# Layer 0's MLP with row weights split one pair ahead and TensorE's order written for all eight first pairs; VectorE's order written at the end of the attention output projection

## The chip, the cores and the metric

The kernel runs on one core of one Trainium2 chip. A core has five engines that work in parallel, each on its own list of instructions in order, and wait for each other by semaphores: TensorE (PE in the profile; its weight loads are PEld), VectorE (DVE), ScalarE (ACT), GpSimd (POOL) and SyncE (SP, which here only issues DMAs). The metric is device time in microseconds (us). Before the change it is 1701.62 us, the median of three runs (1700.1 to 1701.74).

## The reference, cut to what matters

Two sequences of 512 tokens and width 1024 go through the same two layers. Layer 0 mixes tokens by a Fourier transform, layer 1 by attention; each layer ends with a squared-ReLU MLP of width 4096.

```python
def sq_relu_mlp(h, w_up, w_down):
    a = jnp.maximum(h @ w_up, 0)
    return (a * a) @ w_down

def trunk(x, ...):
    for i in range(DEPTH):
        if i % N_MIXERS == 0:
            x = x + fourier_mix(rms_norm(x, fourier_norm[j]), fourier_w_out[j])
        else:
            x = x + gqa_attention(rms_norm(x, attn_norm[j]), ...)
        x = x + sq_relu_mlp(rms_norm(x, mlp_norm[i]), mlp_w_up[i], mlp_w_down[i])
    return rms_norm(x, final_norm)
```

The change touches how the first MLP starts, and how the second MLP's input is prepared at the end of attention's output projection (`o @ w_o`, added to `x`).

## The kernel before, in words

**Matmuls in three parts.** Every float32 operand is split into a high and a low half of type float32r: ScalarE casts the high half (L82), VectorE subtracts it from the original to get the low half (L83). A product of two operands is then three matmuls: high by high, high by low, low by high (L869 in `product`). The first two of the three need only the weight's high half, the third needs its low half. One `product` runs over four 128-blocks, so it is 12 matmuls.

**The MLP's up-projection by pairs.** `first_product(l, blocks, rows, ahead)` takes the 32 blocks of 128 hidden units two at a time, as a *pair*, and uses a seven-product scheme on 2 by 2 blocks (sequences by halves of the width). The activations stand in `blocks.b` under seven names: `b11` and `b21` (sequence 0), `b22`, and the sums `t1` to `t4`. The first two products of a pair, `first()` with `b11` and `second()` with `b21`, need only sequence 0 and the pair's row weights (`row`, loaded by `load`, split by `split_row`). `second()` accumulates into the same PSUM tile as `first()`, after ScalarE has copied `first()`'s result out (L903). The other five are in `rest()`: `t2`, `t3`, `t1`, then `t4` accumulated on the PSUM tile of `t3`, then `b22` accumulated on that of `t1`. VectorE reads each of these tiles before the next product goes on top of it: L947 after `t2`, L951 after `t3`, L960 after `t1`, L969, L978.

Because `b12`, `b22` and the sums come later (they need sequence 1), the kernel runs the first two products of `AHEADS[l]` pairs ahead: eight pairs in layer 0 (p = 0 to 7), six in layer 1. The first four pairs of layer 0 come with their weights already split (`rows`). For pairs 4 to 7 the loop at L1017 loads and splits, runs `first()`, then `second()` of the pair before. Between them, `todo` (a generator, `Blocks.second_sums`) prepares the sums of the activations: normalization (L208), subtractions (L266, L267, L271, L278) and splits (L82, L83). At p = 5 and 6 the loop also prepares pair 0's weight sums (L918, L919, L922, later L930).

**Buffers.** Loaded weights go to tiles `raw` (5 buffers), split weights to `w` (4 buffers), activations to `u` (38), temporaries to `t` (8), results to `ps` (8 PSUM banks). A load can be issued only when a `raw` buffer has been given back by the split that read it.

**What sets the order.** A scheduler places the instructions of each engine, by its own estimate of when operands are there, and the order on each engine is fixed when the program is built. `tc.manual_schedule(engines={...})` keeps the instructions of the named engines within its block in the order in which the code writes them; instructions of other blocks may still come between. In layer 0's loop TensorE's order is written for p = 0 to 4 and left to the scheduler for p = 5 to 7.

**The end of the output projection.** For the second half of the heads (kh = 1), the loop at L1639 computes, for each sequence q and each of eight row blocks fo, 12 matmuls (L77 to L79, `mm3`) and adds them to `x` (VectorE L852, reading PSUM). Then `square` (ScalarE L154, GpSimd adds it to a running sum, L156), `blocks.gain` (ScalarE L196), and every second fo a store (`put_away`). While sequence 1 is at fo = 4 to 7, the four chunks c0 to c3 of sequence 0 are made ready for layer 1's MLP: `blocks.first(c)` normalizes (VectorE L208) and casts the high half (ScalarE L219); `blocks.first_lo(c)` makes the low half (VectorE L224). c0 and c1 are `b11`, c2 and c3 are `b21`. The MLP's first matmuls follow right behind the last project.

Of the kernel before, what the change touches and what calls it, by code (L numbers as in the profile page):

```python
# [40 lines left out]
def trunk_kernel(ctx, tc, x_in, xt_in, y_out, dcos, dsin, feat, rope, gfour, gcol, grow, gfin,  # L41
# [22 lines left out]
    def tm(shape=(P, 512), dt=F32):  # L64
        return tmp.tile(list(shape), dt, tag="t2", name=nm("t"))
# [4 lines left out]
    def ps():  # L70
        return psp.tile([P, 512], F32, tag="ps", name=nm("ps"))
# [4 lines left out]
    def mm3(out, lh, ll, rh, rl, first, last):  # L76
        nc.tensor.matmul(out, lh, rh, start=first, stop=False)  # L77
        nc.tensor.matmul(out, lh, rl, start=False, stop=False)  # L78
        nc.tensor.matmul(out, ll, rh, start=False, stop=last)  # L79
# [30 lines left out]
    def load_w(src, eng=nc.vector, parts=1, home=own):  # L110
        raw = load_raw(src)
        w = home()
        for i in range(parts):
            sl = slice(i * 1024 // parts, (i + 1) * 1024 // parts)
            split(w[0][:, sl], w[1][:, sl], raw[:, sl], eng)
        return w
# [24 lines left out]
    def load_xs(q, src):  # L141
        for i in range(4):
            xs[q, i] = slot([P, 2, 512], F32)
            nc.sync.dma_start(xs[q, i], src[i])

    def xt(q, fo):
        return xs[q, fo // 2][:, fo % 2]

    def square(q, fo, n=512):

        if fo == 0:
            acc[q] = tm()
        s = tm() if fo else acc[q]
        nc.scalar.activation(s[:, :n], xt(q, fo)[:, :n], AF.Square)  # L154
        if fo:
            nc.gpsimd.tensor_add(acc[q][:, :n], acc[q][:, :n], s[:, :n])  # L156
# [25 lines left out]
    def put_away(q, i):  # L182
        nc.sync.dma_start(park[q, i], xs[q, i])
# [482 lines left out]
    ET = mybir.EngineType  # L666
    with tc.manual_schedule(engines={ET.PE, ET.Activation, ET.DVE, ET.Pool, ET.SP}):
# [127 lines left out]
        blocks = Blocks(0)  # L795
# [26 lines left out]
        rows = []  # L822
# [49 lines left out]
    def first_product(l, blocks, rows, ahead):  # L872
# [8 lines left out]
        np_, ah = NPS[l], AHEADS[l]  # L881
# [133 lines left out]
        pairs = [Pair(p) for p in range(np_)]  # L1015
        whole = 2 * np_ == NF
        for p in range(ah):  # L1017
            pair = pairs[p]
            with tc.manual_schedule(engines={ET.PE}) if whole and p < 5 else nullcontext():
                if p < len(rows):  # L1020
                    pair.row = rows[p]
                else:
                    pair.load()
                    pair.split_row()
                pair.first()
                if whole:
                    if p == 3:
                        blocks.root(1)
                        pairs[0].second()
                        pairs[1].second()  # L1030
                        blocks.spread(1)
                        pairs[2].second()
                    elif p > 3:
                        pairs[p - 1].second()
                else:
                    if p > 0:
                        pair.second()
                    if p == 1:
                        pairs[0].second()
                    if p == 2:  # L1040
                        blocks.root(1)
                    if p == 3:
                        blocks.spread(1)
            if p > 3 - whole:
                for _ in range(3 - 2 * l):
                    next(todo, None)
            if whole and p == ah - 1:
                pair.second()
            if 2 * np_ == NF and p == 5:
                pairs[0].load_sums()  # L1050
                pairs[0].sums_23()
            if 2 * np_ == NF and p == 6:
                pairs[0].split_23()
# [62 lines left out]
    def second_product(l, blocks, rows, late=lambda: None, ready=lambda m: None):  # L1116
# [179 lines left out]
        def finish(m):  # L1296
            left[m] -= 1
            if left[m] == 0:
                nc.vector.tensor_add(xs[0, m][:, 1], xs[0, m][:, 1], e[m])
                nc.vector.tensor_add(xs[1, m], xs[1, m], e[m].unsqueeze(1).broadcast_to([P, 2, 512]))  # L1300
                ready(m)

        first_product(l, blocks, rows, ahead)
        e += [tm() for _ in range(4)]
        items, waiting = [], []
# [181 lines left out]
    vt, kr, kT, qr, oT = {}, {}, {}, {}, {}  # L1487
# [70 lines left out]
    for cg in (2, 0, 1):  # L1558
        ws = wkv if cg == 2 else [load_w(w_qkv[cg, u], home=own if u < 2 else lent) for u in range(4)]
# [71 lines left out]
    blocks = Blocks(2 * KC)  # L1631
    nc.scalar.activation(one[:, :1], last[:, :1], AF.Sqrt)
    for kh in range(2):
        ahead += [load_w(w_o[k], home=lent) for k in range(len(ahead), 4 * kh + 4)]
        ws = ahead[4 * kh :]
        for q in range(NSEQ):
            if kh == 0:
                load_xs(q, park[q])
            for fo in range(KC):  # L1639
                project(q, fo, ws, [(oT[q, 4 * kh + k][:, 0], oT[q, 4 * kh + k][:, 1]) for k in range(4)])  # L1640
                if kh == 0:
                    continue
                square(q, fo)
                blocks.gain(q, fo)
                if fo % 2:
                    put_away(q, fo // 2)
                if (q, fo) == (1, 1):
                    blocks.root(0)
                if (q, fo) == (1, 3):
                    blocks.spread(0)  # L1650
                if (q, fo) > (1, 3):
                    blocks.first(fo - 4)
                if (q, fo) > (1, 4):
                    blocks.first_lo(fo - 5)
    blocks.first_lo(3)
    second_product(1, blocks, ())
    ats = []
# [5 lines left out]
    ws = [load_w(w_down[f]) for f in range(NF - 2 * NPS[1])]  # L1663
# [266 lines left out]
```

## Time and profile before

| what | value |
|---|---|
| three runs | 1701.62, 1701.74, 1700.1 us |
| profiled execution's own time | 1699.59 us |
| its span, first to last instruction | 1697.8 us |
| TensorE's granted clock, mean | 0.999 |
| VectorE busy | 1234.2 us (73%) |
| ScalarE busy | 854.9 us (50%) |
| GpSimd busy | 333.4 us (20%) |
| mean DMA traffic | 157 GB/s |
| layer 0's MLP, first matmul | 96.25 us |
| layer 1's MLP, first matmul | 1060.83 us |

All stretches of time below are in microseconds from the start of the span. In a timeline each row has: start, duration, engine, line of the kernel, operation, output and inputs, shape, and a count where rows were merged; in brackets the idle time of the engine just before, and what ended it.

### The profile page before, as it was taken

How to read it: one execution, taken by the hardware profiler on the slowest of the kernel's cores; microseconds unless marked ns; L12 is line 12 of the kernel's file. 1: busy time of each engine (PE TensorE's matmuls, PEld its weight loads, DVE VectorE, ACT ScalarE, POOL GpSimd, SP SyncE). 2: the span in 40 equal slices, each digit the busy share in tenths (PEclk: the TensorE clock that was granted, in tenths of full speed). 3: DMA queues.
4: the chain of work that ended last, by engine and by line, in shares of the span. 5: the costliest groups of instructions: out<-in, count | busy, mean ns of one | idle time of the engine just before them, and what ended most of it. 6: DMA issues, size and time to landing. Idle time of an engine off the chain costs nothing. (4 is left out here: it accounts for less than half of the span.)

```text
span 1697.8 us, 21868 instructions
## 1 busy us (share of the span) xinstructions
PE 1681.2 (99%) x7845; PEld 1395.0 (82%) x7845; DVE 1234.2 (73%) x1809; ACT 854.9 (50%) x1487; POOL 333.4 (20%) x304
## 2 busy tenths in 40 slices
PE   9999999999999999999999999999999999999998
PEld 7987888888788888788888888788888888888887
DVE  8788776557887879876588744687755479787864
ACT  7566444456242424457787714654444544344234
POOL 1321443221000000232344303014422200000002
PEclk9999999999999999999999999999999999999999
DMA  9643555449454644611000213335544686555322
GB/s 337 169 149 113 197 189 182 151 169 390 173 201 146 216 143 175 227 53 34 18 25 1 100 60 127 104 120 195 183 143 154 224 310 229 164 207 189 124 75 100
DMA packets 103679, 265.81 MB, mean 157 GB/s; under 512 B 10177, under 2 KB 10177, under 8 KB 103570
## 3 DMA queue, kind: packets, MB, share of 16 engines
q1 hardware_dynamic: 87410, 232.69, 39.4%
q10 hardware_dynamic: 14256, 25.96, 4.0%
q0 software_dynamic: 1904, 5.77, 1.7%
q8 instruction: 61, 1.00, 0.2%
q14 instruction: 48, 0.39, 0.1%
HBM read 189.40 MB, written 73.92 MB: 155 GB/s over the span
## 5 line engine op out<-in xcount | busy, mean ns | idle before, releaser
L869 PE MATMUL ps<-u,w 128*128 128x512 f32 x4656 | 1065.8, 389 | 4.9 <-DVE w L83 2.5
L869 PEld LDWEIGHTS ps<-u,w 128*128 128x128 f32 x4656 | 872.4, 188 | 189.7 <-DVE w L83 4.1
L82 ACT CAST w<-raw 128x1024 fp32r<-128x1024 f32 (+1 forms) x224 | 217.4, 981 | 444.1 <-PE ps L869 261.4
L83 DVE TENSOR_TENSOR w<-raw,w 128x1024 fp32r<-128x1024 f32 (+1 forms) x224 | 255.1, 1142 | 59.5 <-ACT w L82 59.0
L156 POOL TENSOR_TENSOR t<-t,t 128x512 f32<-128x512 f32 (+1 forms) x56 | 77.6, 1385 | 737.2 <-ACT t L154 681.3
L83 DVE TENSOR_TENSOR u<-u,u 128x1024 fp32r<-128x1024 f32 (+1 forms) x131 | 156.2, 1219 | 21.3 <-ACT u L82 20.6
L82 ACT CAST u<-u 128x1024 fp32r<-128x1024 f32 (+1 forms) x131 | 131.5, 1044 | 72.4 <-PE ps L869 48.8
L77 PE MATMUL ps<-u,u 128*128 128x512 f32 (+2 forms) x388 | 150.2, 387 | 0.4 <-DVE u L83 0.4
L1135 DVE TENSOR_TENSOR u<-ps,u 128x512 f32<-128x512 f32 x160 | 109.5, 686 | 54.0 <-PE ps L869 53.2
L79 PE MATMUL ps<-u,u 128*128 128x512 f32 (+2 forms) x388 | 144.4, 372 | 0.0
L78 PE MATMUL ps<-u,u 128*128 128x512 f32 (+2 forms) x388 | 144.2, 372 | 0.0
L869 PE MATMUL ps<-u,u 128*128 128x512 f32 x576 | 137.6, 390 | 0.6 <-DVE t L960 0.5
L869 PEld LDWEIGHTS ps<-u,u 128*128 128x128 f32 x576 | 107.9, 188 | 24.1 <-issue 0.9
L986 POOL TENSOR_TENSOR u<-u 128x512 f32<-128x512 f32 x28 | 36.6, 1309 | 401.4 <-ACT u L885 401.4
L83 DVE TENSOR_TENSOR u<-ps,u 128x512 fp32r<-128x512 f32 (+4 forms) x118 | 74.7, 649 | 19.6 <-ACT u L82 18.5
L79 PEld LDWEIGHTS ps<-u,u 128*128 128x128 f32 x388 | 73.1, 188 | 13.0
L77 PEld LDWEIGHTS ps<-u,u 128*128 128x128 f32 x388 | 73.3, 189 | 10.7 <-DVE u L83 0.6
L78 PEld LDWEIGHTS ps<-u,u 128*128 128x128 f32 x388 | 73.4, 189 | 10.5
L82 ACT CAST u<-ps 128x512 fp32r<-128x512 f32 (+4 forms) x118 | 65.6, 561 | 27.1 <-PE ps L79 11.6
L947 DVE TENSOR_TENSOR t<-ps,u 128x512 f32<-128x512 f32 x30 | 20.7, 690 | 79.8 <-PE ps L869 58.0
L852 DVE TENSOR_TENSOR u<-ps,u 128x512 f32<-128x512 f32 (+1 forms) x48 | 30.9, 645 | 64.4 <-PE ps L79 64.4
L77 PE MATMUL ps<-u,w 128*128 128x512 f32 (+2 forms) x192 | 65.1, 339 | 0.0
(244 smaller groups left out, 1987.0 us busy)
## 6 DMA issues: line engine op xcount, KB each, us to landing
raw<-w_up SPq DMA_DIRECT2D x82, 512.0 KB, 4.5
u<-spill_t SPq DMA_DIRECT2D x60, 512.0 KB, 5.9
raw<-w_sum SPq DMA_DIRECT2D x56, 512.0 KB, 4.3
u<-spill_b SPq DMA_DIRECT2D x45, 512.0 KB, 5.2
spill_t<-u SPq DMA_DIRECT2D x87, 256.0 KB, 2.0
spill_b<-t ACTq DMA_DIRECT2D x60, 256.0 KB, 3.0
raw<-w_row SPq DMA_DIRECT2D x28, 512.0 KB, 4.1
park<-u SPq DMA_DIRECT2D x24, 512.0 KB, 3.2
```

The source lines that it names most:

```text
L77: nc.tensor.matmul(out, lh, rh, start=first, stop=False)
L78: nc.tensor.matmul(out, lh, rl, start=False, stop=False)
L79: nc.tensor.matmul(out, ll, rh, start=False, stop=last)
L82: nc.scalar.copy(dst_hi, src)
L83: eng.tensor_sub(dst_lo, src, f32(dst_hi))
L156: nc.gpsimd.tensor_add(acc[q][:, :n], acc[q][:, :n], s[:, :n])
L852: nc.vector.tensor_add(x[:, :n], o[:, :n], x[:, :n])
L869: nc.tensor.matmul(o, w[x][:, sl], h[k][y], start=first and k + i == 0, stop=k == n - 1 and i == 2, skip_group_check=not first)
L947: nc.vector.tensor_add(u2, ob, t[:, 0])
L986: eng.tensor_sub(t[:, 0], b12, b11)
L1135: nc.vector.tensor_add(x, o, x)
```

## The change

Two edits. In `first_product`, for layer 0: the block in which TensorE's order is written now covers all eight pairs (p = 0 to 7); pair 4 is loaded and split at its own turn, and pairs 5, 6 and 7 one turn earlier, at the end of the turn of the pair before; and `second()` of the last pair moves from behind the block (and behind a step of `todo`) into it. At the end of the output projection: for sequence 1 and fo = 4 to 7, VectorE's order is the written one, and `first_lo` of the chunk before is written ahead of `first` of the next chunk.

```diff
         for p in range(ah):
             pair = pairs[p]
-            with tc.manual_schedule(engines={ET.PE}) if whole and p < 5 else nullcontext():
+            with tc.manual_schedule(engines={ET.PE}) if whole else nullcontext():
                 if p < len(rows):
                     pair.row = rows[p]
-                else:
+                elif not whole or p == len(rows):
                     pair.load()
                     pair.split_row()
                 pair.first()
...
                     elif p > 3:
                         pairs[p - 1].second()
+                    if len(rows) <= p < ah - 1:
+                        pairs[p + 1].load()
+                        pairs[p + 1].split_row()
+                    if p == ah - 1:
+                        pair.second()
...
-            if whole and p == ah - 1:
-                pair.second()
...
             for fo in range(KC):
-                project(q, fo, ws, [(oT[q, 4 * kh + k][:, 0], oT[q, 4 * kh + k][:, 1]) for k in range(4)])
-                if kh == 0:
-                    continue
-                square(q, fo)
-                blocks.gain(q, fo)
...
-                if (q, fo) > (1, 3):
-                    blocks.first(fo - 4)
-                if (q, fo) > (1, 4):
-                    blocks.first_lo(fo - 5)
+                with tc.manual_schedule(engines={ET.DVE}) if (kh, q) == (1, 1) and fo > 3 else nullcontext():
+                    project(q, fo, ws, [(oT[q, 4 * kh + k][:, 0], oT[q, 4 * kh + k][:, 1]) for k in range(4)])
+                    if kh == 0:
+                        continue
+                    square(q, fo)
+                    blocks.gain(q, fo)
...
+                    if (q, fo) > (1, 4):
+                        blocks.first_lo(fo - 5)
+                    if (q, fo) > (1, 3):
+                        blocks.first(fo - 4)
```

How many instructions each engine has does not change. Their order changes in two stretches only, on each engine; GpSimd's order does not change at all. On SyncE the load of pair 6's row weights now stands ahead of the two loads for pair 0's weight sums, where it stood behind them; the second of these two and a store change places; pair 7's load stays behind them.

**VectorE in layer 0's MLP.** In the kernel before, VectorE has these rows from pair 5's weights (`w_1462`) to pair 6's (`w_1518`); ahead of them, between the split of `w_1417` (pair 4) and here, stand L930 and six rows on activations.

```order
L83 TENSOR_TENSOR w_1462<-raw_1460,w_1462 128x1024
L83 TENSOR_TENSOR u_1410<-u_1406,u_1409 128x1024
L266 TENSOR_TENSOR u_1452<-u_1131,u_885 128x1024
L271 TENSOR_TENSOR u_1089<-u_1174,u_1089 128x1024
L267 TENSOR_TENSOR u_1453<-u_1202,u_1452 128x1024
L271 TENSOR_TENSOR u_1131<-u_1202,u_1131 128x1024
L83 TENSOR_TENSOR w_1518<-raw_1516,w_1518 128x1024
```

With the change the stretch behind the split of `w_1417` begins like this; pair 5's weights are now `w_1451`, pair 6's `w_1498`.

```order
L918 TENSOR_TENSOR raw_1520<-raw_1516,raw_1518 128x512
L919 TENSOR_TENSOR raw_1518<-raw_1518 128x512
L208 TENSOR_TENSOR u_1089<-u_1089,t_1382 128x1024
L208 TENSOR_TENSOR u_1174<-u_1174,t_1382 128x1024
L266 TENSOR_TENSOR u_1405<-u_1089,u_865 128x1024
L83 TENSOR_TENSOR w_1451<-raw_1449,w_1451 128x1024
L267 TENSOR_TENSOR u_1406<-u_1174,u_1405 128x1024
L208 TENSOR_TENSOR u_1131<-u_1131,t_1382 128x1024
L208 TENSOR_TENSOR u_1202<-u_1202,t_1382 128x1024
L83 TENSOR_TENSOR u_1410<-u_1406,u_1409 128x1024
L266 TENSOR_TENSOR u_1457<-u_1131,u_885 128x1024
L83 TENSOR_TENSOR w_1498<-raw_1496,w_1498 128x1024
```

Counted from the first L208, pair 5's low half moves from seventh to fourth place and pair 6's from thirteenth to tenth. L918 and L919 stood before the split of `w_1417` and stand behind it now. Further on, pair 7's low half is the 16th of these rows, and L922 (512 wide) stands just ahead of it; L930 (also 512 wide) stands 11 rows behind it. L947, L951 and L960 of pair 0 now come behind every split of the activation sums; before, L947 stood ahead of the last two of them.

**TensorE in layer 0's MLP.** In the kernel before, these rows follow pair 3's `second()`: pair 5 is `ps_1466`, pair 6 is `ps_1522`; behind the rest of pair 5's `first()` stands all of pair 4's `second()`, and then the rest of pair 6's `first()`.

```order
L869 MATMUL ps_1466<-u_968,w_1462 128x512
L869 MATMUL ps_1466<-u_969,w_1462 128x512
L869 MATMUL ps_1522<-u_968,w_1518 128x512
L869 MATMUL ps_1522<-u_969,w_1518 128x512
L869 MATMUL ps_1466<-u_968,w_1462 128x512 x2
```

With the change pair 5's `first()` and pair 4's `second()` run in one piece each, and then these rows follow: the end of pair 4's `second()` (`ps_1421`), and pair 6 (`ps_1527`).

```order
L869 MATMUL ps_1421<-u_1030,w_1417 128x512
L869 MATMUL ps_1421<-u_1029,w_1417 128x512
L869 MATMUL ps_1527<-u_968,w_1498 128x512
L869 MATMUL ps_1527<-u_969,w_1498 128x512
L869 MATMUL ps_1527<-u_968,w_1498 128x512 x2
```

The matmul that waits for pair 6's low half (the third of its `first()`) is the 63rd behind the transposes of L170 in both orders. Pair 7's third is now the 87th.

**VectorE and TensorE at the end of the output projection.** VectorE before, from the fifth project of sequence 1 (fo = 4) on; L852 adds a project, L208 normalizes a chunk, L224 makes its low half.

```order
L208 TENSOR_TENSOR u_9357<-u_9357,t_9583 128x1024
L852 TENSOR_TENSOR u_9201<-ps_9589,u_9201 128x512
L208 TENSOR_TENSOR u_9395<-u_9395,t_9583 128x1024
L208 TENSOR_TENSOR u_9433<-u_9433,t_9583 128x1024
L852 TENSOR_TENSOR u_9201<-ps_9612,u_9201 128x512
L224 TENSOR_TENSOR u_9610<-u_9357,u_9609 128x1024
L208 TENSOR_TENSOR u_9471<-u_9471,t_9583 128x1024
L852 TENSOR_TENSOR u_9203<-ps_9636,u_9203 128x512
L852 TENSOR_TENSOR u_9203<-ps_9660,u_9203 128x512
L224 TENSOR_TENSOR u_9633<-u_9395,u_9632 128x1024
L224 TENSOR_TENSOR u_9657<-u_9433,u_9656 128x1024
L224 TENSOR_TENSOR u_9681<-u_9471,u_9680 128x1024
```

And with the change:

```order
L852 TENSOR_TENSOR u_9210<-ps_9600,u_9210 128x512
L208 TENSOR_TENSOR u_9366<-u_9366,t_9592 128x1024
L852 TENSOR_TENSOR u_9210<-ps_9626,u_9210 128x512
L224 TENSOR_TENSOR u_9621<-u_9366,u_9620 128x1024
L208 TENSOR_TENSOR u_9404<-u_9404,t_9592 128x1024
L852 TENSOR_TENSOR u_9212<-ps_9653,u_9212 128x512
L224 TENSOR_TENSOR u_9648<-u_9404,u_9647 128x1024
L208 TENSOR_TENSOR u_9442<-u_9442,t_9592 128x1024
L852 TENSOR_TENSOR u_9212<-ps_9680,u_9212 128x512
L224 TENSOR_TENSOR u_9675<-u_9442,u_9674 128x1024
L208 TENSOR_TENSOR u_9480<-u_9480,t_9592 128x1024
L224 TENSOR_TENSOR u_9702<-u_9480,u_9701 128x1024
```

The normalization of c3 moves from ahead of the last two L852 to the last place but one, behind the low half of c2. ScalarE follows with its casts: c1's cast now stands behind fo = 5's square and gain, and c2's and c3's stand as before, c3's behind fo = 7's gain and ahead of the two copies L903 of the MLP's first two pairs.

On TensorE in the same place, the kernel before has 24 matmuls of the MLP (`first()` of pairs 0 and 1) ahead of the first one that reads c2. With the change it has 30: six of pair 2's `first()` (on c0) stand between. In both, that first one is pair 0's `second()`, on the PSUM tile that the first L903 reads.

More of the change, by code (lines that the diff above doesn't have):

```diff
@@ L1639, in trunk_kernel @@
             for fo in range(KC):
-                project(q, fo, ws, [(oT[q, 4 * kh + k][:, 0], oT[q, 4 * kh + k][:, 1]) for k in range(4)])
-                if kh == 0:
-                    continue
-                square(q, fo)
-                blocks.gain(q, fo)
[L1645 to L1650, printed above, removed]
-                if (q, fo) > (1, 3):
-                    blocks.first(fo - 4)
-                if (q, fo) > (1, 4):
-                    blocks.first_lo(fo - 5)
+                with tc.manual_schedule(engines={ET.DVE}) if (kh, q) == (1, 1) and fo > 3 else nullcontext():
[4 more added lines that the diff above has]
+                    blocks.gain(q, fo)
+                    if fo % 2:
+                        put_away(q, fo // 2)
+                    if (q, fo) == (1, 1):
+                        blocks.root(0)
+                    if (q, fo) == (1, 3):
+                        blocks.spread(0)
+                    if (q, fo) > (1, 4):
+                        blocks.first_lo(fo - 5)
+                    if (q, fo) > (1, 3):
+                        blocks.first(fo - 4)
     blocks.first_lo(3)
```

## The prediction, on record before the changed kernel ran

> **What bounds the kernel now.** The page's busy times come first, then TensorE's list of waits (who it waited for, us in total, times, the longest).
>
> ```profile
> PE 1681.2 (99%) x7845; PEld 1395.0 (82%) x7845; DVE 1234.2 (73%) x1809; ACT 854.9 (50%) x1487; POOL 333.4 (20%) x304
> PE ps L869 <- DVE w L83: 2.5, 2, 1.5
> PE ps L869 <- DVE u L224: 0.9, 1, 0.9
> ```
>
> TensorE is busy for 99% of the span and gets no work less, so the change can only close or open waits of TensorE. It reorders two places, and each has one wait before it: one of L83's two (1.5 us) at the start of layer 0's MLP, and L224's (0.9 us) where layer 1's MLP begins. Removing both whole would bring some 2.4 us of idle time, 0.14%. I forecast that the first mostly goes and that the second gives way to a longer one behind it.
>
> **Place 1, layer 0's first pairs.** Timeline of TensorE, then of VectorE.
>
> ```profile
> 114.43 14.34 PE L869 MATMUL ps<-u,w 128*128 128x512 f32 x62
> 130.28 24.43 PE L869 MATMUL ps<-u,w 128*128 128x512 f32 x106 [1.52 <-DVE w L83]
> 154.55 2.88 PE L869 MATMUL ps<-u,u 128*128 128x512 f32 x12
> 157.27 11.04 PE L869 MATMUL ps<-u,w 128*128 128x512 f32 x48
> 168.15 2.88 PE L869 MATMUL ps<-u,u 128*128 128x512 f32 x12
> ...
> 113.12 1.23 DVE L83 TENSOR_TENSOR w<-raw,w 128x1024 fp32r<-128x1024 f32 x1 [2.70 <-ACT w L82]
> 118.80 1.22 DVE L208 TENSOR_TENSOR u<-u,t 128x1024 f32<-128x1024 f32 x1
> 129.02 1.21 DVE L83 TENSOR_TENSOR w<-raw,w 128x1024 fp32r<-128x1024 f32 x1
> 145.00 0.68 DVE L918 TENSOR_TENSOR raw<-raw,raw 128x512 f32<-128x512 f32 x1
> 145.60 2.35 DVE L83 TENSOR_TENSOR u<-u,u 128x1024 fp32r<-128x1024 f32 x2
> 149.38 0.69 DVE L951 TENSOR_TENSOR t<-ps,t 128x512 f32<-128x512 f32 x1 [0.22 <-PE ps L869]
> ```
>
> 48 matmuls take 157.27 to 168.15, so one takes 0.2267 us. The 63rd from 114.43 could start at 114.43 + 62 x 0.2267 = 128.5; it starts at 130.28, as pair 6's low half ends (129.02 + 1.21 = 130.23).
>
> With the change VectorE's pace decides. Between 118.80 and 129.02 lie nine steps of 1024 elements: 1.135 each. A 512 step takes 145.60 - 145.00 = 0.60. Pair 4's split still starts at 113.12; L918 and L919 follow at 114.26 and end their slots at 115.55 (two times 0.60, and 0.1 as the second waits for the first). Pair 6's low half is the tenth from there: 115.55 + 9 x 1.135 + 1.22 = 127.0, and TensorE wants it at 128.5. Pair 7's (14 wide steps and L922 ahead) starts at 115.55 + 14 x 1.135 + 0.60 = 132.0 and ends at 133.3. TensorE wants it as 87th, at 114.43 + 86 x 0.2267 = 133.9: on time, but by 0.6 only.
>
> Late is L951, which must read `t3`'s tile before `t4` goes on top. Ahead of it VectorE now has 27 wide steps and six of 512, with 0.1 for one more dependent pair: 115.55 + 30.65 + 3.6 + 0.1 = 149.9, done at 150.6 instead of 150.1. TensorE would reach `t4` as the 157th, at 149.8, so it waits until 150.6, and starts `b22`, 12 matmuls on, at 150.6 + 2.72 = 153.35. Before it was 154.55. **Term 1: -1.2 us.** Its ends: nothing, if VectorE slips by 1.2 us more over its 33 steps, and -1.8 (130.28 - 128.5), if L951 is on time. I take the worked-out middle, since both paces are read off.
>
> The loads are hidden: pair 7's `raw` buffer comes free with pair 5's split, at 115.55 + 3 x 1.135 + 1.22 = 120.2; the loads of `raw` in this stretch landed within
>
> ```profile
> DMA to landing us min/median/max: 3.5/4.1/5.7
> ```
>
> so by 126, and VectorE splits it from 132.0 on. ScalarE's casts and copies, each 1.04 or 0.6 us and in the new order, I placed likewise; the tightest, the copy of pair 6's `first()`, is late by 0.3 us ahead of the same L951 wait.
>
> **Place 2, the end of the output projection.** TensorE (among 48 single rows the last matmul of fo = 4 and of fo = 7), VectorE, GpSimd, ScalarE:
>
> ```profile
> 1052.44 0.39 PE L79 MATMUL ps<-u,u 128*128 128x512 f32 x1
> 1060.60 0.39 PE L79 MATMUL ps<-u,u 128*128 128x512 f32 x1
> 1060.83 2.20 PE L869 MATMUL ps<-u,w 128*128 128x512 f32 x9
> 1063.93 11.93 PE L869 MATMUL ps<-u,w 128*128 128x512 f32 x51 [0.90 <-DVE u L224]
> 1075.70 0.95 PE L162 MATMUL ps<-ones,t 128*128 128x2 f32 x8
> ...
> 1052.21 1.40 DVE L208 TENSOR_TENSOR u<-u,t 128x1024 f32<-128x1024 f32 x1 [1.84 <-ACT t L171]
> 1054.14 3.45 DVE L208 TENSOR_TENSOR u<-u,t 128x1024 f32<-128x1024 f32 x2
> 1059.24 2.31 DVE L208 TENSOR_TENSOR u<-u,t 128x1024 f32<-128x1024 f32 x1
> 1062.67 1.21 DVE L224 TENSOR_TENSOR u<-u,u 128x1024 fp32r<-128x1024 f32 x1
> 1066.49 1.86 DVE L224 TENSOR_TENSOR u<-u,u 128x1024 fp32r<-128x1024 f32 x1 [0.37 <-ACT u L219]
> 1072.93 1.23 DVE L83 TENSOR_TENSOR w<-raw,w 128x1024 fp32r<-128x1024 f32 x1 [4.58 <-ACT w L82]
> ...
> 1051.24 1.29 POOL L156 TENSOR_TENSOR t<-t,t 128x512 f32<-128x512 f32 x1 [1.45 <-ACT t L154]
> 1055.07 1.43 POOL L156 TENSOR_TENSOR t<-t,t 128x512 f32<-128x512 f32 x1 [2.54 <-ACT t L154]
> 1059.05 1.41 POOL L156 TENSOR_TENSOR t<-t,t 128x512 f32<-128x512 f32 x1 [2.55 <-ACT t L154]
> 1062.96 4.30 POOL L156 TENSOR_TENSOR t<-t,t 128x512 f32<-128x512 f32 x2 [2.50 <-ACT t L154]
> ...
> 1054.29 0.63 ACT L154 ACTIVATE t<-u 128x512 f32<-128x512 f32 x1 [2.12 <-issue]
> 1054.83 0.71 ACT L196 ACTIVATE u<-u,gc 128x512 f32<-128x512 f32 x1
> 1065.42 1.04 ACT L219 CAST u<-u 128x1024 fp32r<-128x1024 f32 x1
> 1066.36 0.57 ACT L903 COPY u<-ps 128x512 f32<-128x512 f32 x1
> ```
>
> Before, nine matmuls from 1060.83 end their slots at 1062.87, and the tenth starts at 1063.93, when c1's low half is done (1062.67 + 1.21). Loss: 1.06 us. c3 causes none.
>
> The four L208 last 1.40, twice 1.72 and 2.31 where 1.22 is plain. Each slow one ends 1.09 us behind a GpSimd add: 1052.53 and 1053.61, 1056.50 and 1057.59, 1060.46 and 1061.55. So a VectorE operation on two SBUF inputs waits for the whole add. Where both want to start, the add that stood waiting goes first: the add requested at 1055.07 ran between two back-to-back L208. The Trainium skill ("SBUF — State Buffer", section "Who interferes with whom") calls this an exclusive lock between VectorE and GpSimd, held for the whole instruction. By that rule the sum below stands; with shared bandwidth in its place, the first rival would.
>
> Now the new chain, with ScalarE's rows for its steps (square 0.63, 0.15 on to the add; cast 1.04) and 1.26 for an add that waited. fo = 4 ends at 1052.83, and its projects follow every 2.72.
> - c0: L208 1053.5 to 1054.7; L852 of fo = 5 waits for TensorE until 1055.6; L224 1056.2 to 1057.4.
> - The add of fo = 5 stands ready from 1057.1, takes 1057.3 to 1058.6, and c1's L208 ends at 1059.7. L852, cast (to 1060.75), L224 to 1062.0. TensorE wants it at 1060.83 + 7 x 0.2267 = 1062.4: **the old wait is gone.**
> - The add of fo = 6 goes first again (1061.95 to 1063.2): c2's L208 ends at 1064.3, L852 at 1064.95, the cast at 1065.35, L224 at 1066.6.
> - The add of fo = 7 goes first again (1066.55 to 1067.8): c3's L208 ends at 1068.9, its cast at 1070.0.
>
> Behind that cast, on ScalarE in order, stand the two L903 copies; the first ends at 1070.0 - 0.1 + 0.57 = 1070.5 (before: 1066.93). Without it TensorE can't put pair 0's `second()` on that tile. That is its 31st matmul, wanted at 1060.83 + 30 x 0.2267 = 1067.6. Wait: 2.85 us; c3's low half (1071.2) is then on time for the 40th. **Term 2: 2.85 - 1.06 = +1.8 us.** Its ends: -1.06, no wait, if the adds don't get in; +3.1, if one more add (1.26) gets in.
>
> VectorE then has time: before, its next work came 4.58 us later, on its own cast, and moves along with TensorE.
>
> **Sum.** -1.2 + 1.8 = +0.6 us. The profiled execution took 1699.59, so its like would take 1700.2. The median of the runs shown lies 2.0 us above it; on that, 1701.62 + 0.6 = **1702.2 us**.
>
> **Rivals.**
> - *The adds don't get in.* If VectorE's back-to-back operations keep GpSimd out, c1 to c3 come some 1.26 us earlier each, c3's cast ends by 1066.5 and no wait is left: -1.2 - 1.06 = -2.3, 1699.3 us. Against it stand the two adds at 1055.07 and 1059.05 that got in. 13%.
> - *The pair ahead brings nothing* (L951 late by 1.2 us more): +1.8, 1703.4 us. 10%.
> - *The clock falls in the new wait.* Stretches of TensorE at the span's end (length, busy and matmuls, granted clock, DMA share, GB/s):
>
> ```profile
> 1690.00:1691.00 1.00, 0.15 (x2) 1.00 0.37 141
> 1692.00:1693.00 1.00, 0.00 (x0) 1.00 0.31 117
> 1693.00:1694.00 1.00, 0.00 (x0) 0.51 0.68 262
> ```
>
>   TensorE stopped at 1690.15, and its clock halved at about 1693.0, 2.85 us later. The new wait leaves it idle for 2.7. If the clock falls and takes as long to return, half of 2.85 us is lost: +0.6 + 1.4 = +2.0, 1703.6 us. For it: the two lengths nearly meet; against: it must be the worst phase. 9%. The Trainium skill ("TensorE: Matmul & The Clock Gate", section "HAM oscillation — how this bites in real kernels") warns only of gaps above some 3.4 us. By that rule the clock stays, though this trace shows it fall earlier.
> - *Slower: pair 7's load is late.* It is issued at 120.2 and cast and split must follow, with VectorE's list in order behind it. Its split is due at 132.0 and its cast (1.04) by then, so a landing up to 130.9 (10.7 us) is free; then L951, and TensorE with it, shifts one for one. To be over 0.2% slower (3.4 us) it needs 2.8 more: a landing after 13.5 us. Nothing in this stretch took over 5.7. 4%, at 1705.5 us.
>
> **How the numbers follow.** The forecast has 60% (between -0.8 and +2.0 us), the rivals 13, 10, 9 and 4; 4% is for what I don't see. A measurement of this kernel can tell about 0.2%, 3.4 us, from no change; only the last rival and part of the unseen lie beyond. Faster 0.03, same 0.92, slower 0.05. The range takes in the first three rivals and the spread of the runs (1700.1 to 1701.74): 1699.0 to 1704.4.
>
> **What would show it.** Right: the wait for L83 near 129 is gone and a short wait for VectorE's L951 stands near 150; layer 1's wait for L224 is gone, and one of 2.6 to 2.9 us for ScalarE's L903 stands some 7 us behind the MLP's first matmul; c1 to c3's L208 last over 2 us. Wrong: no wait there, L208 at 1.22, or a clock below 1.00.

## The result, and the profile after

| | before | after |
|---|---|---|
| median of 22 runs each, us | 1700.08 (1699.27 to 1701.74) | 1702.82 (1700.88 to 1704.48) |
| ratio after to before, 95% interval | | 1.0015 [1.0009, 1.0021] |
| profiled execution, us (span) | 1699.59 (1697.8) | 1702.27 (1700.5) |
| layer 0's MLP: first matmul to the `b22` product, us | 58.30 | 57.73 |
| layer 1's MLP: first matmul to the sums L162, 60 matmuls, us | 14.87 | 18.12 |

The change costs 0.15%, 2.6 us (the interval is 1.5 to 3.6). The last two rows account for it: -0.57 in the first place and +3.25 in the second make +2.7, as the spans do (1700.5 - 1697.8).

The page's busy times after, and the two rows of TensorE's list of waits (us in total, times, the longest) that answer to those shown of before:

```profile
PE 1683.3 (99%) x7845; PEld 1396.5 (82%) x7845; DVE 1230.9 (72%) x1809; ACT 854.0 (50%) x1487; POOL 333.4 (20%) x304
PE ps L869 <- ACT u L903: 3.3, 2, 2.6
PE ps L869 <- DVE w L83: 1.0, 1, 1.0
```

Both waits that were aimed at are gone: the 1.5 us one for L83 (the one of 1.0 stood before too) and the 0.9 us one for L224. In their place stand two waits for ScalarE's copies L903. TensorE's busy time grew by 2.1 us with as many matmuls: most of that is no wait, but a lower clock, worked out under place 2.

**Place 1.** Timelines of TensorE, ScalarE and VectorE in layer 0 after:

```profile
114.52 23.57 PE L869 MATMUL ps<-u,w 128*128 128x512 f32 x101
138.78 15.48 PE L869 MATMUL ps<-u,w 128*128 128x512 f32 x67 [0.69 <-ACT u L903]
154.10 2.88 PE L869 MATMUL ps<-u,u 128*128 128x512 f32 x12
...
130.65 0.33 ACTq L879 DMA_DIRECT2D spill_b<-u  x1
131.02 0.59 ACT L903 COPY u<-ps 128x512 f32<-128x512 f32 x1 [0.40 <-ACT u L885]
...
137.12 0.63 ACT L885 ACTIVATE u<-u 128x512 f32<-128x512 f32 x1
137.78 0.33 ACTq L879 DMA_DIRECT2D spill_b<-u  x1
138.14 0.58 ACT L903 COPY u<-ps 128x512 f32<-128x512 f32 x1 [0.40 <-ACT u L885]
...
126.03 1.22 DVE L83 TENSOR_TENSOR w<-raw,w 128x1024 fp32r<-128x1024 f32 x1
132.31 1.21 DVE L83 TENSOR_TENSOR w<-raw,w 128x1024 fp32r<-128x1024 f32 x1
150.19 0.68 DVE L951 TENSOR_TENSOR t<-ps,t 128x512 f32<-128x512 f32 x1
```

VectorE went as worked out: pair 6's low half is done at 127.25 (forecast 127.0), pair 7's is begun at 132.31 (132.0), L951 at 150.19 (149.9). TensorE waits for something else: at 138.78 for pair 6's copy L903, which stands on ScalarE behind the squares of another pair (their second step, L885) and the issue of a spill store (L879, which sends the squares to memory). That issue holds ScalarE's list for 0.40 us, as the bracket at the copy shows.

**Place 2.** TensorE, then VectorE's normalizations of c1 to c3, GpSimd's last three adds, ScalarE's last cast and the two copies, and stretches of 1 us (length; busy time and count of PE, PEld, DVE, ACT, POOL; granted clock; DMA share; GB/s):

```profile
1060.09 6.96 PE L869 MATMUL ps<-u,w 128*128 128x512 f32 x30
1069.66 8.71 PE L869 MATMUL ps<-u,w 128*128 128x512 f32 x30 [2.62 <-ACT u L903]
1078.21 0.95 PE L162 MATMUL ps<-ones,t 128*128 128x2 f32 x8
...
1056.59 2.31 DVE L208 TENSOR_TENSOR u<-u,t 128x1024 f32<-128x1024 f32 x1
1061.16 2.31 DVE L208 TENSOR_TENSOR u<-u,t 128x1024 f32<-128x1024 f32 x1
1065.73 2.32 DVE L208 TENSOR_TENSOR u<-u,t 128x1024 f32<-128x1024 f32 x1
...
1056.41 1.41 POOL L156 TENSOR_TENSOR t<-t,t 128x512 f32<-128x512 f32 x1 [1.30 <-ACT t L154]
1060.66 1.73 POOL L156 TENSOR_TENSOR t<-t,t 128x512 f32<-128x512 f32 x1 [2.84 <-ACT t L154]
1065.23 1.74 POOL L156 TENSOR_TENSOR t<-t,t 128x512 f32<-128x512 f32 x1 [2.84 <-ACT t L154]
...
1068.08 1.04 ACT L219 CAST u<-u 128x1024 fp32r<-128x1024 f32 x1 [2.38 <-DVE u L208]
1069.03 1.06 ACT L903 COPY u<-ps 128x512 f32<-128x512 f32 x2
...
1069.00:1070.00 1.00, 0.34 (x1) 0.34 (x2) 0.84 (x1) 1.00 (x3) 0.00 (x0) 0.83 0.00 0
1070.00:1071.00 1.00, 1.00 (x3) 0.81 (x3) 0.38 (x1) 0.10 (x1) 0.00 (x0) 0.50 0.00 0
1073.00:1074.00 1.00, 1.00 (x6) 0.82 (x5) 0.00 (x0) 0.00 (x0) 0.00 (x0) 0.96 0.00 0
```

Each of the three normalizations lasts some 2.31 us, where c0's, ahead of them, lasts 1.22, and ends 1.08 us behind a GpSimd add that got in ahead of it. TensorE wants its 31st matmul at 1060.09 + 30 x 0.2267 = 1066.89 and gets it at 1069.66: 2.77 us. Then its clock halves. A granted clock of 0.83 in one us means 0.34 us at half: it fell at 1069.66, and by the same reckoning rose again at 1073.08, 3.42 us later. The 30 matmuls behind the wait take 1078.21 - 1069.66 = 8.55 in place of 6.80.

### The profile page after: what moved, and what is told of

It is laid out like the page before. It is cut to its first block, busy times and chain, and to the rows that moved or that the text cites. A ratio compares the mean times of both kernels' runs of the same rounds, so it can differ in the third digit from the quotient of the medians.

```text
span 1700.5 us, 21863 instructions
## 1 busy us (share of the span) xinstructions
PE 1683.3 (99%) x7845; PEld 1396.5 (82%) x7845; DVE 1230.9 (72%) x1809; ACT 854.0 (50%) x1487; POOL 333.4 (20%) x304
## 5 line engine op out<-in xcount | busy, mean ns | idle before, releaser
L83 DVE TENSOR_TENSOR w<-raw,w 128x1024 fp32r<-128x1024 f32 (+1 forms) x224 | 255.3, 1143 | 60.7 <-ACT w L82 60.2
L83 DVE TENSOR_TENSOR u<-u,u 128x1024 fp32r<-128x1024 f32 (+1 forms) x131 | 156.4, 1220 | 23.6 <-ACT u L82 23.0
L83 DVE TENSOR_TENSOR u<-ps,u 128x512 fp32r<-128x512 f32 (+4 forms) x118 | 74.8, 650 | 19.5 <-ACT u L82 18.3
L852 DVE TENSOR_TENSOR u<-ps,u 128x512 f32<-128x512 f32 (+1 forms) x48 | 31.0, 645 | 67.5 <-PE ps L79 67.5
L947 DVE TENSOR_TENSOR t<-ps,u 128x512 f32<-128x512 f32 x30 | 20.7, 690 | 79.4 <-PE ps L869 57.3
```

The costliest lines, as they stand in the source:

```text
L83: eng.tensor_sub(dst_lo, src, f32(dst_hi))
L947: nc.vector.tensor_add(u2, ob, t[:, 0])
```

## The experiments

Theory from the two traces: the first edit brings 0.6 us; the second costs 1.7 us of wait, because GpSimd's adds get in and c3's cast, with the copies behind it, comes late; and that wait lets the clock fall, for some 1.6 us more. Each kernel was run 11 times beside the kernel before, two firsts 6 times.

| kernel | median, us | ratio to before, 95% interval |
|---|---|---|
| first edit alone | 1699.07 | 0.9995 [0.9986, 1.0004] |
| second edit alone | 1702.99 | 1.0018 [1.0009, 1.0027] |
| three adds out | 1698.37 | 0.9988 [0.9979, 0.9996] |
| three firsts | 1699.67 | 0.9998 [0.9989, 1.0006] |
| four firsts | 1697.64 | 0.9985 [0.9976, 0.9994] |
| four firsts, old VectorE order | 1698.57 | 0.9990 [0.9981, 0.9999] |
| copies first | 1701.90 | 1.0010 [1.0001, 1.0018] |
| four firsts and copies first | 1697.15 | 0.9984 [0.9975, 0.9992] |
| two firsts | 1705.53 | 1.0032 [1.0020, 1.0044] |
| written order, not ahead | 1701.40 | 1.0008 [1.0000, 1.0017] |

**The first edit alone.** The changed kernel with the old loop at the end of the output projection.

```diff
-                with tc.manual_schedule(engines={ET.DVE}) if (kh, q) == (1, 1) and fo > 3 else nullcontext():
...
-                    if (q, fo) > (1, 4):
-                        blocks.first_lo(fo - 5)
-                    if (q, fo) > (1, 3):
-                        blocks.first(fo - 4)
+                if (q, fo) > (1, 3):
+                    blocks.first(fo - 4)
+                if (q, fo) > (1, 4):
+                    blocks.first_lo(fo - 5)
```

> The first edit alone (layer 0's pairs); the end of the output projection is that of the kernel before. Theory (the first edit brought some 0.6 us, the second cost 3.3): 0.6 us below the kernel before, ratio 0.9993 to 1.0000; TensorE's wait for L224 of 0.9 us is back, no wait for L903 in layer 1, the granted clock stays 1.00 from 1060 to 1080; in layer 0 the b22 product starts some 0.6 us earlier than before, and a wait for L903 near 138 stays. Rival (the first edit brought nothing or cost something, and the whole loss is elsewhere): 0 to +2 us, b22 no earlier than before. Had term 1 been sized right: -1.2 us.

Measured: 1.1 us below before, with an interval that takes in both zero and the expected 0.6. The trace decides the sizes: `b22` starts 57.76 us behind the MLP's first matmul (58.30 before, so 0.54 gained), layer 1's 60 matmuls take 14.86 us as before, and the clock stays at 1.00 there.

**The second edit alone.** The kernel before with the lines above the other way round.

> The second edit alone (VectorE's order at the end of the output projection); layer 0 is that of the kernel before. Theory (wait plus clock): 3.2 us above the kernel before, ratio 1.0013 to 1.0025: a wait of 2.7 to 2.9 us for L903 some 7 us behind the MLP's first matmul (1.7 us net of the old wait), and behind it some 3 us at half the granted clock, which cost another 1.5. Rival (the clock's fall in the profile belongs to that one execution, not to the edit): the wait is there, the clock stays, and the time is 1.7 us above, ratio about 1.0010.

TensorE in the profiled execution, and the clock in two stretches of 4 us:

```profile
1060.73 6.96 PE L869 MATMUL ps<-u,w 128*128 128x512 f32 x30
1070.31 7.11 PE L869 MATMUL ps<-u,w 128*128 128x512 f32 x30 [2.62 <-ACT u L903]
1077.26 0.95 PE L162 MATMUL ps<-ones,t 128*128 128x2 f32 x8
...
1068.00:1072.00 4.00, 1.69 (x7) 1.34 (x8) 1.92 (x2) 2.02 (x3) 0.00 (x0) 1.00 0.00 0
1072.00:1076.00 4.00, 4.00 (x19) 3.30 (x19) 0.61 (x1) 2.06 (x3) 0.00 (x0) 1.00 0.02 4
```

The same wait of 2.62 us as in the changed kernel, and here the clock stays up: 30 matmuls take 6.95 us, and the span is 1.8 us over that of before, the wait alone. But this execution took 1701.40, and the median is 1702.99: the profiled execution alone looks as the rival has it. Each run also lists its mean granted clock, and 3.4 us at half take 0.001 from it (3.4 x 0.5 / 1700). The four runs at 0.999 took 1701.40 to 1702.40; the seven at 0.998 or 0.997 have a median of 1704.02. So the clock falls in some executions of one kernel and not in others, and it costs some 2 us when it does. In the changed kernel 21 of 22 runs are at 0.998 or 0.997; of 82 runs of the kernel before, 72 are at 0.999. The mean also takes in a fall at the end of the span, so it counts the falls in the middle only roughly. The theory holds for the median, with the fall as a matter of chance.

**Three adds out.** The adds that got in, taken away.

```diff
-        if fo:
+        if fo and add:
             nc.gpsimd.tensor_add(acc[q][:, :n], acc[q][:, :n], s[:, :n])
...
-                    square(q, fo)
+                    square(q, fo, add=q == 0 or fo < 5)
```

> The changed kernel without GpSimd's adds of fo = 5, 6 and 7 for sequence 1 in the second half of the output projection: three of eight blocks are left out of sequence 1's sum of squares, which scales layer 1's MLP. Theory (the adds that stand waiting get in between VectorE's back-to-back operations and hold it): L208 of c1 to c3 last 1.2 us in place of 2.3; c3's cast ends near 1065.6 in place of 1069.1; the copy L903 is done by 1066.5, TensorE wants it at 1066.9, so neither the wait nor the fall of the clock is left: 4.5 us below the changed kernel, 1.8 below the kernel before (ratio 0.9985 to 0.9995). Rival (VectorE's written order itself delays c3, whatever GpSimd does): L208 still 2.3 us, the wait of 2.6 us stays, ratio 1.0010 or more.

TensorE, the last normalization, the last cast and the copies:

```profile
1059.66 13.76 PE L869 MATMUL ps<-u,w 128*128 128x512 f32 x60
...
1063.12 1.22 DVE L208 TENSOR_TENSOR u<-u,t 128x1024 f32<-128x1024 f32 x1
1064.37 1.05 ACT L219 CAST u<-u 128x1024 fp32r<-128x1024 f32 x1 [1.28 <-DVE u L208]
1065.33 1.06 ACT L903 COPY u<-ps 128x512 f32<-128x512 f32 x2
```

All 60 matmuls run in one piece, L208 is back at 1.22, and the time is 1.8 us below before, as expected. VectorE's order was the same, so it is the adds.

**Three firsts.** The same late copy, but 36 matmuls ahead of it.

```diff
-            with tc.manual_schedule(engines={ET.PE}) if whole else nullcontext():
+            with tc.manual_schedule(engines={ET.PE}) if whole or p < 3 else nullcontext():
...
-                    if p > 0:
-                        pair.second()
-                    if p == 1:
-                        pairs[0].second()
                     if p == 2:
+                        pairs[1].second()
+                        pairs[0].second()
                         blocks.root(1)
+                    if p > 1:
+                        pair.second()
```

> The changed kernel with 36 matmuls in place of 30 (first() of three whole pairs) ahead of the first second() in layer 1's MLP; nothing else changes, and the copies on ScalarE end no earlier. So the idle stretch of TensorE is shortened to some 1.8 us (1068.3 to 1070.0). Theory (the clock fell because TensorE stood idle for 2.6 us, and a shorter stretch leaves it up): the granted clock stays 1.00; 2.7 us below the changed kernel, level with the kernel before (ratio 0.9995 to 1.0005). Rival (the clock falls at this place, or at any wait, whatever its length): half clock for some 3 us again, only 1.0 us below the changed kernel, ratio 1.0008 to 1.0015.

```profile
1059.77 8.32 PE L869 MATMUL ps<-u,w 128*128 128x512 f32 x36
1069.83 5.73 PE L869 MATMUL ps<-u,w 128*128 128x512 f32 x24 [1.74 <-ACT u L903]
```

In this timeline of TensorE the 24 matmuls behind a wait of 1.74 us take 1075.40 (where L162 starts) - 1069.83 = 5.57: no lower clock. All 11 runs are at 0.999 and lie within 1.1 us (1699.36 to 1700.44); the changed kernel's spread over 3.6. The time is 0.5 us below before, level within the interval, as expected: 0.9 us less of wait made some 3.2 us less time than in the changed kernel.

**Two firsts.** The stretch lengthened: 24 matmuls, all four pairs' order in one written block.

```diff
+                    if p == 3:
+                        with tc.manual_schedule(engines={ET.PE}):
+                            pairs[0].first()
+                            pairs[1].first()
+                            pairs[0].second()
+                            pairs[1].second()
+                            pairs[2].first()
+                            pairs[2].second()
...
```

> The changed kernel with 24 matmuls (first() of two pairs) in place of 30 ahead of the first second() in layer 1's MLP, the rest as it was. So TensorE's idle stretch is lengthened to some 4.1 us (1065.5 to 1069.6). Theory (the clock falls at some moment between 2.6 and 5.7 us after TensorE stops, as at the ends of the spans so far, so that a stretch of 2.8 us meets it in most executions and one of 4.1 us too, while one of 1.7 us never does): the clock falls again, stays at half for some 3.4 us, and costs up to 1.7; the wait is 1.4 us longer: 1.4 us above the changed kernel, 4.1 above the kernel before, ratio 1.0018 to 1.0030, mean clock 0.998 or less in nearly all runs. Rival (the clock's time at half grows with the idle stretch, or the fall is over before TensorE restarts): ratio below 1.0015 or above 1.0035.

```profile
1061.01 5.60 PE L869 MATMUL ps<-u,w 128*128 128x512 f32 x24
1070.56 10.06 PE L869 MATMUL ps<-u,w 128*128 128x512 f32 x36 [3.95 <-ACT u L903]
1081.30 3.02 PE L869 MATMUL ps<-u,w 128*128 128x512 f32 x12 [0.68 <-ACT u L903]
...
1070.00:1071.00 1.00, 0.44 (x1) 0.42 (x2) 0.94 (x1) 1.00 (x3) 0.00 (x0) 0.84 0.00 0
1074.00:1075.00 1.00, 1.00 (x5) 0.77 (x4) 0.00 (x0) 0.00 (x0) 0.00 (x0) 0.95 0.00 0
```

The clock fell at 1070.68, 4.07 us behind the end of the matmuls, and rose at 1074.10: 3.42 us again, so its time at half does not grow with the stretch. All six runs are at 0.998. The ratio lies just above the range of the theory, and the time is 5.3 us over before where 4.1 was expected: the wait of 0.68 at 1081.30, for pair 2's copy right behind its `first()`, came with my new order and I had not counted it; the other 0.5 stays open. The expectation also misread the ends of the spans: there the fall came 2.06 us (four firsts with the old order) to 5.19 us (first edit alone) behind TensorE's last matmul, not 2.6 to 5.7.

**Four firsts.** 48 matmuls and L162 ahead of the first `second()`: enough to cover the copy.

```diff
-            with tc.manual_schedule(engines={ET.PE}) if whole else nullcontext():
+            with tc.manual_schedule(engines={ET.PE}) if whole or p < 4 else nullcontext():
...
-                if whole:
-                    if p == 3:
...
+                if p == 3:
+                    blocks.root(1)
+                    pairs[0].second()
+                    pairs[1].second()
+                    blocks.spread(1)
+                    pairs[2].second()
+                elif p > 3:
+                    pairs[p - 1].second()
```

> The changed kernel with first() of four whole pairs (48 matmuls) and sequence 1's sum (L162) ahead of the first second() in layer 1's MLP. Theory (the second edit's own gain of 1.06 us is real, and only TensorE's order uncovered the late copy): TensorE is busy until 1071, the copy ends at 1070, so neither the old wait for L224 nor the new one for L903 is there, and the clock stays 1.00: 1.7 us below the kernel before (0.6 from layer 0, 1.06 here), ratio 0.9985 to 0.9995, all runs within 2 us of each other. Rival (a later wait takes its place, at the transposes behind L162 or at the copies of the other pairs): level with the kernel before, with a new wait between 1071 and 1085.

```profile
1060.33 11.04 PE L869 MATMUL ps<-u,w 128*128 128x512 f32 x48
1071.21 0.95 PE L162 MATMUL ps<-ones,t 128*128 128x2 f32 x8
1072.02 5.75 PE L869 MATMUL ps<-u,w 128*128 128x512 f32 x24
```

TensorE runs through. 2.6 us below before, within 1.0 us of each other in 11 runs: some 0.9 more than expected, which the interval (0.9976 to 0.9994, 4.1 to 1.0 us below) does not resolve.

**Four firsts with VectorE's old order.** As above, with the loop of the first experiment.

> The kernel of the four firsts with VectorE's order at the end of the output projection as it was before: only TensorE's order in layer 1 and the first edit differ from the kernel before. Theory (VectorE's written order is what takes the 0.9 us wait for c1's low half away): the wait for L224 of 0.9 us is there again, no wait for L903, time 0.6 us below the kernel before, 1.1 above the kernel of the four firsts with the new order. Rival (TensorE's order alone removes that wait): level with the four firsts with the new order.

```profile
PE ps L869 <- DVE u L224: 0.9, 1, 0.9
```

The wait for c1's low half is back in TensorE's list, and the time is 0.9 us over the four firsts, with runs that hardly overlap (1698.00 to 1699.16, and 1697.07 to 1698.06). Against the kernel before, the time is 1.6 us less where 0.6 was expected; the interval (3.2 to 0.2 us below) takes in both, and the difference stays open. So the second edit does remove the wait that it was aimed at; it cost time only because TensorE's order left the copy uncovered.

**Copies first.** ScalarE's order written for pairs 5 to 7 of layer 0, with the next pair's cast ahead of this pair's copy.

```diff
-            with tc.manual_schedule(engines={ET.PE}) if whole else nullcontext():
+            with tc.manual_schedule(engines={ET.PE, ET.Activation} if p > 4 else {ET.PE}) if whole else nullcontext():
...
+                if whole and len(rows) <= p < ah - 1:
+                    pairs[p + 1].load()
+                    pairs[p + 1].split_row()
                 pair.first()
...
-                    if len(rows) <= p < ah - 1:
-                        pairs[p + 1].load()
-                        pairs[p + 1].split_row()
```

> The changed kernel with ScalarE's order written too for pairs 5 to 7 of layer 0 (the next pair's cast, then this pair's copy L903, then the squares of the pair before). Theory (term 1 fell short because ScalarE's copies stood behind squares and the issues of spill stores; VectorE's L951 is the next limit, as the prediction had it): TensorE's wait for L903 near 138 is gone, a wait for L951 of some 0.5 to 0.9 us stands near 151, and the b22 product starts 57.2 us behind the MLP's first matmul (57.73 in the changed kernel, 58.30 before); the time falls by 0.5 us against the changed kernel, which is below what the runs tell (ratio to before 1.0005 to 1.0020). Rival (ScalarE is simply full, and the copies come as late in any order): the wait near 138 stays within 0.2 us, b22 at 57.7.

```profile
114.65 35.91 PE L869 MATMUL ps<-u,w 128*128 128x512 f32 x156
150.94 3.01 PE L869 MATMUL ps<-u,w 128*128 128x512 f32 x12 [0.38 <-DVE t L951]
153.79 2.43 PE L869 MATMUL ps<-u,u 128*128 128x512 f32 x10
...
129.50 0.58 ACT L903 COPY u<-ps 128x512 f32<-128x512 f32 x1
136.36 0.57 ACT L903 COPY u<-ps 128x512 f32<-128x512 f32 x1
```

Pair 5's copy comes 1.5 us earlier (129.50 for 131.02), pair 6's 1.8 (136.36 for 138.14). TensorE runs 156 matmuls in one piece and then waits for L951 only (0.38 us, a little less than expected), as term 1 of the prediction had it; the `b22` product starts 153.79 - 96.45 = 57.34 us behind the first matmul. Place 2 is the changed kernel's, wait and fall of the clock included. The time is 1.7 us over before, as expected; the 0.4 us of place 1 against the changed kernel (57.73 - 57.34) is below what the runs tell.

**Written order, not ahead.** The kernel before, with only TensorE's order written for all eight pairs.

```diff
-            with tc.manual_schedule(engines={ET.PE}) if whole and p < 5 else nullcontext():
+            with tc.manual_schedule(engines={ET.PE}) if whole else nullcontext():
...
+                    if p == ah - 1:
+                        pair.second()
...
-            if whole and p == ah - 1:
-                pair.second()
```

> The kernel before with TensorE's order written for all eight pairs of layer 0, and with nothing loaded or split one pair ahead; the output projection is that of the kernel before. It tells which half of the first edit brought its 0.55 us. Theory (the split one pair ahead did: it moves the low halves forward on VectorE): TensorE's wait for pair 6's low half near 130 is still 1.5 us, b22 starts 58 us or more behind the MLP's first matmul (58.30 before, 57.73 changed), time level with the kernel before, ratio 0.9995 to 1.0008. Rival (TensorE's written order did): that wait is below 0.5 us, and b22 starts by 57.8.

```profile
130.84 6.64 PE L869 MATMUL ps<-u,w 128*128 128x512 f32 x28 [1.49 <-DVE w L83]
138.79 17.98 PE L869 MATMUL ps<-u,w 128*128 128x512 f32 x78 [1.31 <-DVE w L83]
```

The old wait stays, and a second one for pair 7's low half comes behind it: `b22` starts 59.80 us behind the first matmul, 1.5 later than before. The median is 1.2 us over before, at the upper end of the expected range (the interval begins at no change); the profiled execution is the slowest of the eleven, because the clock fell in it at another place (last section). So the written order alone brings nothing and costs in the trace, and the gain of the first edit needs the split one pair ahead. That split without the written order was not run.

**Four firsts and copies first** together:

> The four firsts in layer 1 and ScalarE's written order in layer 0 together. If both theories hold: 1.7 + 0.5 = 2.2 us below the kernel before, ratio 0.9982 to 0.9992, no wait for L903 in either MLP, granted clock 1.00 throughout. Rival: one of them takes back what the other gives, level with the kernel before.

Measured 3.0 us below before, 0.5 below the four firsts; no wait for L903 is left in TensorE's list, and the clock is 1.00 in layer 1's start. It is the fastest kernel here (ratio 0.9984 [0.9975, 0.9992]), though the interval does not part it from the four firsts alone.

## Why the prediction was right, and where it was not

The time was forecast as 1702.2 and is 1702.82, within the range, and "the same within 0.2%" is what came. But two errors meet in that: the three runs that I built on (1701.62) lay 1.5 us above the median of 22 (1700.08), and the difference that I forecast, +0.6, lies below the interval of the measured one (1.5 to 3.6). That the number came so close is luck. The likeliest case did not come; the rival of the falling clock (+2.0) did. Of the prediction's own signs, L903's wait and the slow L208 came, the short wait for L951 did not, and one sign of being wrong did: "a clock below 1.00".

- **Term 2, the wait: right.** 2.85 us forecast, 2.77 measured; less the old 1.06 it is +1.7 (+1.8). Each link is there: the adds in front of c1's, c2's and c3's normalization, L208 at 2.31, the old wait gone, c3's low half never waited for. The run without the adds shows the cause, and the four firsts show what the edit is worth with the copy covered.
- **The clock: the step that failed.** I priced it well (1.4; 8.55 - 6.95 against the run where it stayed up is 1.6), but gave it 9%, because "it must be the worst phase". It needs no such thing: by their mean clock it fell in nearly all runs of the changed kernel, and the last section shows that some 2 us idle within one window of 3.41 are enough. The one row that I had, 2.85 us from TensorE's stop to the fall at the span's end, I read as the least time that it takes. Now there are shorter ones: 2.61 us here (1060.09 + 6.96 to 1069.66). The Trainium skill ("TensorE: Matmul & The Clock Gate", section "HAM oscillation — how this bites in real kernels") warns of gaps above some 3.4 us only; here a gap of 2.62 us was enough, so the measurement decides against that bound.
- **Term 1: the mechanism right, the size half.** -1.2 forecast, -0.57 measured. VectorE's part held to 0.3 us. The step that failed is "ScalarE's casts and copies [...] I placed likewise; the tightest [...] is late by 0.3 us": pair 6's copy was 1.4 us late for TensorE (wanted at 114.52 + 101 x 0.2267 = 137.42, started 138.78); some 0.4 us of that was lost before, at pair 5's copy. What I left out are the issues of spill stores on ScalarE's own list, 0.40 us each, one ahead of either copy; they alone don't make up the 1.1 us, and the rest was not parted. With the copies first the gain is 58.30 - 57.34 = 0.96, and L951 is the limit, as forecast.
- **The other rivals.** The adds did get in. Pair 7's load was on time (its split began at 132.31). The pair ahead brought something: with the written order but without it, place 1 is 1.5 us worse than before.

## What to carry to other kernels

When a written order moves a producer, follow the whole list of the engine behind it: here c3's cast was not late for its own reader, but for the copies queued behind it, and TensorE's list had only 30 matmuls to cover them. A wait of two to three us on TensorE has to be priced with the clock that may fall behind it, which here doubled its cost; the spread of the runs and their mean clock show that better than one profile. And on an engine that also issues DMAs, count each issue as work.

## What the runs showed of the hardware that I had not expected

- **The clock's fall.** Worked out as above, it lasted from 1069.94 to 1073.34 in the copies-first kernel, and in the written-order kernel, at another place, from 712.26 to 715.66, behind a wait of TensorE for L1135:

```profile
710.86 7.36 PE L869 MATMUL ps<-u,w 128*128 128x512 f32 x24 [2.12 <-DVE u L1135]
...
712.00:713.00 1.00, 1.00 (x5) 0.76 (x4) 1.00 (x3) 0.26 (x1) 1.00 (x1) 0.63 0.86 311
715.00:716.00 1.00, 1.00 (x5) 0.83 (x4) 1.00 (x2) 0.00 (x0) 0.00 (x0) 0.67 0.44 176
```

  There TensorE had been running for 1.4 us when the clock fell. All four last 3.40 to 3.42 us. A gap of 1.74 us had no fall in 11 runs, the one of 2.12 had one in the single profile that shows it, one of 2.62 in most runs. That fits a clock that is set every 3.41 us by how idle the stretch behind was, some 2 us being enough, at a phase that has nothing to do with the program. The profiles bear this out, because the clock falls once more at the end of each span. These rows are of the changed kernel and of the written-order kernel:

```profile
1697.00:1698.00 1.00, 0.00 (x0) 0.00 (x0) 0.00 (x0) 0.00 (x0) 0.00 (x0) 0.86 0.39 150
1698.00:1699.00 1.00, 0.00 (x0) 0.00 (x0) 0.41 (x2) 0.25 (x1) 0.00 (x0) 0.85 0.07 25
```

  By the same reckoning these falls came at 1697.72 and 1698.70, which is 628.06 and 986.44 us behind the first fall of the same execution: 184 times 3.4134 us, and 289 times 3.4133. In the two firsts (628.06) and the copies-first kernel (628.04) it is 184 times again, although the fall came 4.87, 2.67 and 4.32 us behind TensorE's last matmul in the changed kernel, the two firsts and the copies-first kernel.

  I call each such stretch of 3.41 us a window. In all twelve profiles, with the windows counted from each one's own falls, a clock that was up fell at the end of every window with 2.02 us of idle TensorE or more, and of none with 1.77 or less (the first 13 us of the spans left out, as the record of the clock does not cover them).

  It explains the second edit alone, too: in its profile a window ended at 1068.77 (the fall at 1696.82, less 184 x 3.4133) and cut the wait into 1.08 and 1.54 us, so the clock stayed up. At a random phase a wait of 2.62 us would meet the fall in 58 to 73% of executions. This is an estimate, (3.41 - 2.62 + 2 x (2.62 - 2.02)) / 3.41, and the same with 1.77. The 7 of 11 of the second edit alone fit; the 21 of 22 of the changed kernel are more, and that stays open.

  The Trainium skill ("TensorE: Matmul & The Clock Gate", section "What's actually happening") has such a window, 3413 ns long and free-running, and the traces agree with both; that a whole window must be idle does not agree.
- **GpSimd's add goes first.** In all nine cases seen here (three each in the changed kernel, the second edit alone and the three firsts) an add that became ready while VectorE worked got in ahead of VectorE's next operation on two SBUF inputs, which then lasted 2.31 us in place of 1.22.
